# Opening of a two-layer encoder kernel: half of the first shift's weights multiplied with c on TensorE, and rows of u put ahead of the first weights' casts

## The chip, the cores and the metric

The kernel runs on one core of one Trainium2 chip. The metric is the device time of one execution in microseconds (us); lower is better. Besides the timed runs there is one profiled execution of the kernel, whose trace is read here. In the rows PE is TensorE (matrix products), PEld its weight loads, DVE is VectorE, ACT is ScalarE, POOL is GpSimd, and SP is the engine whose queue issues most transfers.

## What is computed

Two layers with three sub-layers each work on x (256 rows of 1024) under a conditioning vector c. Every sub-layer has a shift, a scale and a gate of 1024 numbers each, all of them products of silu(c) with a slice of `mod_w`:

```python
cs = jax.nn.silu(c)
for layer in range(DEPTH):
    mod = (cs @ mod_w[layer] + mod_b[layer]).reshape(bsz, N_SUB, 3, D_MODEL)
    x = adaln_sublayer(x, mod[:, 0], lambda u: 0.5 * swiglu(u, ffn_w_gate[layer, 0], ...), ...)
    ...

def adaln_sublayer(x, m, f, ln_g, ln_b):
    shift, scale, gate = m[:, None, 0], m[:, None, 1], m[:, None, 2]
    y = f(x * (1 + scale) + shift)
    return layer_norm(DEEPNORM_ALPHA * x + (1 + gate) * y, ln_g, ln_b)
```

The first sub-layer's f is a SwiGLU: silu(u @ w_gate) * (u @ w_up), times w_down. Nothing of it can start before u = x * (1 + scale) + shift is there, and that needs the whole scale and the whole shift of sub-layer 0.

## The kernel before

**The modulation.** `mod_gen` is a generator that walks through all slices of `mod_w`, for each sub-layer first scale (i = 1), then shift (i = 0), then gate (i = 2). A slice is 1024 x 1024 and comes in eight pieces k = 0 to 7, each 128 partitions by 1024. VectorE multiplies a piece by column k of c (`csT`) and adds it to an accumulator of 128 x 1024 (L219 for k = 0, L226 after that). When all eight are in, the partitions have still to be summed: `mod_cols0` does that with eight products on TensorE, in each of which a block of 128 x 128 of the accumulator is the loaded weight and a single column of ones is what moves through; so 1024 sums come out as eight columns of 128. In the trace each such fp32 product appears as two weight loads and two matmuls, so a group of eight products is "x16".

The first shift is a special case. Its piece k = 5 does not go over VectorE: TensorE multiplies it directly with column 5 of c (`self.share = self.mod_cols0(w, c)`, also eight products), two wide products that only keep TensorE active follow (`warm`, 512 columns each, result unused), and VectorE takes k = 0 to 4, 6 and 7. Then come the eight products with ones over the accumulator, in two PSUM banks in turn, and after each two of them VectorE adds their columns to B. `A` (scale + 1) and `B` (shift) are set by `mod_scale` and `mod_shift` behind VectorE's last accumulating step.

**The first u.** `make_u` with both row blocks (`joint`): TensorE turns x by products with the identity into four PSUM banks (L290). For each of four row groups of u (k0 = 0, 2, 4, 6) `affine` applies A and B, half on VectorE (L304) and half on ScalarE (L306), and `split` makes two fp32r parts of the result: a rounded copy on ScalarE (CAST, L266) and the rest by a subtraction on VectorE or GpSimd (L267). Three products of such parts stand for one fp32 product.

**The first weights.** `ffn` with `first == "start"` loads the first chunk of w_gate and w_up in two halves s = 0 and 1. The s = 0 halves are split in pieces of four k each, on ScalarE (cast) and GpSimd (subtraction): the two of w_gate at once where they stand in the program, the two of w_up from the list `between`, from which `make_u` takes one after each of the first two row groups. Then the products of chunk 0 start (L548), and after them chunk 1, whose w_up weights are loaded into a buffer that comes free when the s = 1 half of w_gate is split.

Each engine works off its instructions in the order in which they are recorded, and a scheduler chooses that order by what is ready; `behind(mark)` keeps an instruction behind another. Transfers go through SP's queue in order, each waiting until its buffer is free: `w8` (three buffers of 1 MB, the pairs of pieces and the FFN weights) and `wd` (three buffers of 512 KB, the single pieces and w_down).

Of the kernel before, what the change touches and what calls it, by code (L numbers as in the profile page):

```python
# [18 lines left out]
P = 128  # L19
# [14 lines left out]
class Trunk:  # L34
# [108 lines left out]
    def mod_cols0(self, acc, c, use=None):  # L143

        pts = [self.bank("gu", (P, KD)) for _ in range(2 if use else 1)]
        for k in range(KD):
            pt = pts[k // 2 % len(pts)]
            self.last_col = self.nc.tensor.matmul(pt[:, k : k + 1], acc[:, k * P : (k + 1) * P], c,
                                                  start=True, stop=True)
            if use and k % 2:  # L150
                use(slice(k - 1, k + 1), pt)
        return pts[0]
# [13 lines left out]
    def mod_shift(self, si, acc):  # L166
# [3 lines left out]
        if si == 0:  # L170
            self.mod_cols0(acc, self.one[:, 0:1], lambda c, pt: add(B[:, c], pt[:, c], B[:, c]))
        else:
            add(B, B, b)
            add(B, B, self.mod_cols(acc))
# [11 lines left out]
    def mod_gen(self):  # L186
# [4 lines left out]
        ws, loaded, G, step = {}, 0, None, None  # L191
# [14 lines left out]
        for n, (si, i, k) in enumerate(todo):  # L206
# [10 lines left out]
            w, c = ws.pop((si, i, k)), self.cs[:, k : k + 1]  # L217
            if k == 0:
                nc.vector.tensor_scalar_mul(acc, w, c)  # L219
            elif (si, i, k) == (0, 0, 5):  # L220
                self.share = self.mod_cols0(w, c)
                with self.behind(self.last_col):
                    for _ in range(2):
                        self.warm(self.x[:, 0, 0:512])
            else:
                step = nc.vector.scalar_tensor_tensor(acc, w, c, acc, ALU.mult, ALU.add)  # L226
# [3 lines left out]
            if self.last_mm is not None and self.si == 3:  # L230
# [3 lines left out]
                with self.behind(self.last_mm):  # L234
                    self.mod_sums(si, i, acc, G, step)
            else:
                self.mod_sums(si, i, acc, G, step)
            self.mdone.add((si, i))
            yield 0
            if si == 0 and i == 1:  # L240
                self.setup_bias()
                self.load_x()

    def mod_sums(self, si, i, acc, G, step):
# [7 lines left out]
        else:  # L252
            if not si:
                with self.behind(step):
                    self.mod_scale(si, self.scale)
                    self.nc.vector.tensor_tensor(out=self.AB[0][1], in0=self.share[:, 0:KD], in1=self.bcol[:, 0, 0],
                                                 op=ALU.add)
# [1288 lines left out]
```

## Time and profile before

| | before |
|---|---|
| median of 3 runs | 1204.01 us (1203.51 to 1205.42) |
| the profiled execution: time, span | 1207.6 us, 1205.8 us |
| PE busy | 1130.7 us, 94% of the span |
| DVE busy | 914.1 us, 76% |
| ACT busy | 548.5 us, 45% |
| POOL busy | 254.7 us, 21% |
| transfers | 259.74 MB, mean 215 GB/s |

The span is the time between the first and the last instruction in the trace; the time of the execution is a little longer. Busy shares are means over stages that have different limits, so the opening has to be read by itself: in the first 17 us TensorE does almost nothing.

### The profile page before, as it was taken

What the parts mean: (1) busy time and instruction counts of PE and PEld (TensorE: products, weight loads), DVE (VectorE), ACT (ScalarE), POOL (GpSimd) and SP (SyncE); (2) the same over time, 40 slices, a digit from 0 to 9 for tenths busy, and PEclk for the clock granted to TensorE, in tenths of its full rate; (3) what the DMA queues carried; (4) which work ended last, traced back from release to release, by engine and by line L of the source; (5) the groups of instructions that cost most, each with busy time, mean ns of one, the idle gap of its engine ahead of it and who ended that gap; (6) DMA issues with size and microseconds to landing.
All of it is one profiled execution on the core that took longest, in us unless ns stands there. A gap on an engine that the chain in (4) does not pass through costs nothing.

```text
span 1205.8 us, 19555 instructions
## 1 busy us (share of the span) xinstructions
PE 1130.7 (94%) x7703; PEld 1023.8 (85%) x7703; DVE 914.1 (76%) x1404; ACT 548.5 (45%) x963; POOL 254.7 (21%) x186
## 2 busy tenths in 40 slices
PE   4998999999799998999999899999898998999997
PEld 3887999789687887998999799999887878899995
DVE  6699777698886677878876778878799748866545
ACT  0644434356432445544443553444356656544430
POOL 0631000224731362230000332000121234400001
PEclk9998999999999999999999999999999998999999
DMA  9779998454310577689988388988733335885620
GB/s 354 256 255 327 314 318 294 142 181 132 106 36 1 192 258 231 205 286 300 323 291 302 98 275 291 301 300 281 257 129 124 112 105 192 295 259 174 214 73 35
DMA packets 155333, 259.74 MB, mean 215 GB/s; under 512 B 8813, under 2 KB 117354, under 8 KB 155242
## 3 DMA queue, kind: packets, MB, share of 16 engines
q1 hardware_dynamic: 155050, 258.45, 64.3%
q8 instruction: 60, 0.98, 0.3%
q14 instruction: 31, 0.25, 0.1%
q10 hardware_dynamic: 192, 0.05, 0.0%
HBM read 257.43 MB, written 1.05 MB: 214 GB/s over the span
## 4 chain that ended last, share of the span: by engine, by line
PE 61%; DVE 21%; DMA 7%; ACT 4%; issue 4%; POOL 3%; SPq 0%; POOLq 0%; DVEq 0%; ACTq 0%
PE gu L272 10%; PE gu L271 10%; PE gu L273 10%; PE acc L273 7%; PE acc L271 7%; PE acc L272 7%; DMA wd<-ffn_w_down 3%; DVE macc L226 2%; DVE g L267 2%; DMA wd<-mod_w 2%; DVE x L391 1%; DMA w<-ffn_w_up 1%; DVE u L267 1%; POOL hd L267 1%; DVE k L1043 1%
## 5 line engine op out<-in xcount | busy, mean ns | idle before, releaser
L226 DVE SCALAR_TENSOR_TENSOR macc<-wd,csT,macc 128x1024 f32<-128x1024 f32 x112 | 167.8, 1498 | 26.3 <-DMA wd<-mod_w 26.0
L271 PE MATMUL gu<-uT,g 128*128 128x256 f32 x640 | 181.3, 283 | 2.5 <-ACT sg L556 2.5
L273 PE MATMUL gu<-uT,g 128*128 128x256 f32 x640 | 181.4, 283 | 1.7 <-DVE g L267 1.7
L273 PE MATMUL gu<-uT,u 128*128 128x256 f32 x640 | 181.3, 283 | 1.0 <-DVE u L267 1.0
L271 PE MATMUL gu<-uT,u 128*128 128x256 f32 x640 | 181.2, 283 | 0.0
L272 PE MATMUL gu<-uT,u 128*128 128x256 f32 x640 | 181.2, 283 | 0.0
L272 PE MATMUL gu<-uT,g 128*128 128x256 f32 x640 | 181.1, 283 | 0.0
L266 ACT CAST hd<-wd 128x1024 fp32r<-128x1024 f32 x88 | 92.2, 1049 | 139.4 <-DMA wd<-ffn_w_down 127.0
L271 PE MATMUL acc<-hd,h 128*128 128x512 f32 x352 | 142.0, 403 | 1.9 <-ACT h L266 1.9
L273 PE MATMUL acc<-hd,h 128*128 128x512 f32 x352 | 138.9, 395 | 2.5 <-DVE h L267 2.5
L272 PE MATMUL acc<-hd,h 128*128 128x512 f32 x352 | 138.9, 394 | 0.0
L267 DVE TENSOR_TENSOR g<-w,g 128x1024 fp32r<-128x1024 f32 x86 | 118.2, 1377 | 26.6 <-ACT g L266 26.5
L271 PEld LDWEIGHTS gu<-uT,g 128*128 128x128 f32 x640 | 122.7, 192 | 4.6 <-ACT sg L556 3.2
L273 PEld LDWEIGHTS gu<-uT,g 128*128 128x128 f32 x640 | 122.7, 192 | 2.4 <-DVE g L267 2.4
L273 PEld LDWEIGHTS gu<-uT,u 128*128 128x128 f32 x640 | 122.9, 192 | 1.2 <-DVE u L267 1.2
L272 PEld LDWEIGHTS gu<-uT,g 128*128 128x128 f32 x640 | 122.7, 192 | 1.4
L272 PEld LDWEIGHTS gu<-uT,u 128*128 128x128 f32 x640 | 122.9, 192 | 0.0
L271 PEld LDWEIGHTS gu<-uT,u 128*128 128x128 f32 x640 | 122.9, 192 | 0.0
L267 DVE TENSOR_TENSOR u<-w,u 128x1024 fp32r<-128x1024 f32 x81 | 104.0, 1289 | 21.5 <-ACT u L266 21.1
L266 ACT CAST u<-w 128x1024 fp32r<-128x1024 f32 (+1 forms) x89 | 91.6, 1038 | 58.8 <-DMA w<-ffn_w_up 44.6
L267 POOL TENSOR_TENSOR hd<-wd,hd 128x1024 fp32r<-128x1024 f32 x32 | 86.6, 2712 | 149.0 <-ACT hd L266 149.0
L267 POOL TENSOR_TENSOR hl<-w,hl 128x1024 fp32r<-128x1024 f32 x28 | 72.7, 2607 | 202.6 <-ACT hl L266 202.1
(403 smaller groups left out, 2472.8 us busy)
## 6 DMA issues: line engine op xcount, KB each, us to landing
wd<-mod_w SPq DMA_DIRECT2D x130, 512.0 KB, 5.0
wd<-ffn_w_down SPq DMA_DIRECT2D x88, 512.0 KB, 4.7
w<-ffn_w_gate SPq DMA_DIRECT2D x43, 1024.0 KB, 8.4
w<-ffn_w_up SPq DMA_DIRECT2D x43, 1024.0 KB, 7.3
w<-hyb_w_in SPq DMA_DIRECT2D x16, 1024.0 KB, 5.9
w<-mod_w SPq DMA_DIRECT2D x7, 1024.0 KB, 7.5
w<-hyb_w_out SPq DMA_DIRECT2D x4, 1024.0 KB, 4.9
w<-mla_w_out SPq DMA_DIRECT2D x4, 1024.0 KB, 5.0
```

The lines of the kernel that those rows point to most:

```text
L226: step = nc.vector.scalar_tensor_tensor(acc, w, c, acc, ALU.mult, ALU.add)
L266: i = self.nc.scalar.copy(hi, src)
L267: return i, (eng or self.nc.vector).tensor_tensor(out=lo, in0=src, in1=hi.bitcast(F32), op=ALU.subtract)
L271: nc.tensor.matmul(out, lh, rh, start=first, stop=False)
L272: nc.tensor.matmul(out, lh, rl, start=False, stop=False)
L273: self.last_mm = nc.tensor.matmul(out, ll, rh, start=False, stop=last)
L391: V.tensor_tensor(out=x[:, b, sl], in0=tmp, in1=x[:, b, sl], op=ALU.add)
L1043: nc.vector.scalar_tensor_tensor(y[:, d:], pt[:, : S - d], tap(3 - d), y[:, d:], ALU.mult, ALU.add)
```

## The change

Pieces k = 4 to 7 of the first shift go over TensorE instead of VectorE. A new function `mod_direct` makes eight products for each: the piece is the weight that is loaded, column k of c moves, and the results add up in PSUM in two banks. VectorE keeps k = 0 to 3; its accumulator goes into the same banks by eight products with ones, ahead of k = 4. After each two products of k = 7 VectorE adds the bias into B. The separate share of k = 5, its two wide products and the closing eight products with ones are gone. `mod_scale` for sub-layer 0 moves up behind `setup_bias`, one wide product stands behind the last column instead of two, and all four splits of the first weights now stand behind row groups of u: one after the first, two after the second, one after the third.

```diff
--- before.py
+++ after.py
@@ -140,16 +140,25 @@
             nc.vector.tensor_reduce(out=out[:, k0 : k0 + 4], in_=pt, op=ALU.add, axis=AX.X)
         return out
 
-    def mod_cols0(self, acc, c, use=None):
-
-        pts = [self.bank("gu", (P, KD)) for _ in range(2 if use else 1)]
+    def mod_cols0(self, acc, c):
+
+        pt = self.bank("gu", (P, KD))
         for k in range(KD):
-            pt = pts[k // 2 % len(pts)]
-            self.last_col = self.nc.tensor.matmul(pt[:, k : k + 1], acc[:, k * P : (k + 1) * P], c,
-                                                  start=True, stop=True)
-            if use and k % 2:
-                use(slice(k - 1, k + 1), pt)
-        return pts[0]
+            self.nc.tensor.matmul(pt[:, k : k + 1], acc[:, k * P : (k + 1) * P], c, start=True, stop=True)
+        return pt
+
+    def mod_direct(self, w, c, first, last):
+
+        nc = self.nc
+        if first:
+            self.direct = [self.bank("gu", (P, KD)) for _ in range(2)]
+        for k in range(KD):
+            pt = self.direct[k // 2 % 2]
+            self.last_col = nc.tensor.matmul(pt[:, k : k + 1], w[:, k * P : (k + 1) * P], c, start=first and k in (0, 2),
+                                             stop=last, skip_group_check=True)
+            if last and k % 2:
+                two = slice(k - 1, k + 1)
+                nc.vector.tensor_tensor(out=self.AB[0][1][:, two], in0=pt[:, two], in1=self.bcol[:, 0, 0, two], op=ALU.add)
 
     def mod_scale(self, si, sums):
         nc = self.nc
@@ -167,11 +176,8 @@
         nc = self.nc
         B, b = self.AB[si][1], self.bcol[:, si, 0]
         add = lambda out, x, y: nc.vector.tensor_tensor(out=out, in0=x, in1=y, op=ALU.add)
-        if si == 0:
-            self.mod_cols0(acc, self.one[:, 0:1], lambda c, pt: add(B[:, c], pt[:, c], B[:, c]))
-        else:
-            add(B, B, b)
-            add(B, B, self.mod_cols(acc))
+        add(B, B, b)
+        add(B, B, self.mod_cols(acc))
 
     def mod_gate(self, si, acc, G):
 
@@ -188,7 +194,7 @@
         nc, t = self.nc, self.t
         self.AB, self.G = {}, {}
         todo = [(si, i, k) for si in range(len(self.subs)) for i in (1, 0, 2) for k in range(KD)]
-        ws, loaded, G, step = {}, 0, None, None
+        ws, loaded, G = {}, 0, None
 
         def load(si, i, k):
             l, j = self.subs[si]
@@ -215,15 +221,15 @@
                 load(*todo[loaded])
                 loaded += 1
             w, c = ws.pop((si, i, k)), self.cs[:, k : k + 1]
+            direct = (si, i) == (0, 0) and k >= KD // 2
             if k == 0:
                 nc.vector.tensor_scalar_mul(acc, w, c)
-            elif (si, i, k) == (0, 0, 5):
-                self.share = self.mod_cols0(w, c)
-                with self.behind(self.last_col):
-                    for _ in range(2):
-                        self.warm(self.x[:, 0, 0:512])
+            elif direct:
+                self.mod_direct(w, c, False, k == KD - 1)
             else:
-                step = nc.vector.scalar_tensor_tensor(acc, w, c, acc, ALU.mult, ALU.add)
+                nc.vector.scalar_tensor_tensor(acc, w, c, acc, ALU.mult, ALU.add)
+            if (si, i, k) == (0, 0, KD // 2 - 1):
+                self.mod_direct(acc, self.one[:, 0:1], True, False)
             yield 1
             if k < KD - 1:
                 continue
@@ -232,16 +238,17 @@
                 self.held = self.last_mm
                 yield 0
                 with self.behind(self.last_mm):
-                    self.mod_sums(si, i, acc, G, step)
+                    self.mod_sums(si, i, acc, G)
             else:
-                self.mod_sums(si, i, acc, G, step)
+                self.mod_sums(si, i, acc, G)
             self.mdone.add((si, i))
             yield 0
             if si == 0 and i == 1:
                 self.setup_bias()
+                self.mod_scale(0, self.scale)
                 self.load_x()
 
-    def mod_sums(self, si, i, acc, G, step):
+    def mod_sums(self, si, i, acc, G):
         if i == 2:
             self.mod_gate(si, acc, G)
         elif i == 1:
@@ -249,12 +256,7 @@
                 self.mod_scale(si, self.mod_cols(acc))
             else:
                 self.scale = self.mod_cols0(acc, self.one[:, 0:1])
-        else:
-            if not si:
-                with self.behind(step):
-                    self.mod_scale(si, self.scale)
-                    self.nc.vector.tensor_tensor(out=self.AB[0][1], in0=self.share[:, 0:KD], in1=self.bcol[:, 0, 0],
-                                                 op=ALU.add)
+        elif si:
             self.mod_shift(si, acc)
 
     def need(self, *key):
@@ -315,14 +317,13 @@
             next(self.todo[0])
             self.need(si, 0)
             with self.behind(self.last_col):
-                for _ in range(2):
-                    self.warm(n[:, 0, 0:512])
-            for k0 in range(0, KD, 2):
-                with self.behind(self.marks[1]):
+                self.warm(n[:, 0, 0:512])
+            for k0, weights in zip(range(0, KD, 2), ((0,), (2, 1), (3,), ())):
+                with self.behind(*self.marks[1:2]):
                     affine(k0, pts[k0 // 2])
-                if k0 < 4:
+                for i in weights:
                     with self.behind(self.marks[1]):
-                        self.marks[1:] = self.between[k0 // 2]()
+                        self.marks[1:] = self.between[i]()
         else:
             for k0 in range(0, KD, 2):
                 affine(k0, rows(k0))
@@ -518,10 +519,7 @@
                             continue
                         for k in (slice(0, 4), slice(4, 8)):
                             piece = lambda hl=hl, r=r, k=k: self.split(hl[:, 0, k], hl[:, 1, k], r[:, k], nc.gpsimd)
-                            if g:
-                                self.between.append(piece)
-                            else:
-                                self.marks[1:] = piece()
+                            self.between.append(piece)
                     if not s:
                         yield
             u = self.u
```

On TensorE the place is the opening, between the transposes of x and the first products of chunk 0. `gu` are PSUM banks, `x` the input, `G` the accumulator, `w` and `wd` pieces of weights, `uT` the first u. Before:

```order
L125 MATMUL gu_146<-x_118,ident 128x512
L148 MATMUL gu_156<-csT,w_23_153 128x1 [waits DMAHW6_49]
L148 MATMUL gu_156<-csT,w_23_153 128x1 x7
L125 MATMUL gu_165<-x_118,ident 128x512 [waits Activation_49]
L125 MATMUL gu_167<-x_118,ident 128x512 [waits PE_49]
L148 MATMUL gu_195<-one,G_120 128x1 [waits DVE_49,PE_49]
...
L125 MATMUL gu_209<-x_118,ident 128x512
L125 MATMUL gu_211<-x_118,ident 128x512
L548 MATMUL gu_243<-uT_124,g_184 128x256 [waits DVE_49,Activation_49]
```

And in the changed kernel, with the rows between the first two of each group of eight left out:

```order
L125 MATMUL gu_149<-x_121,ident 128x512
L157 MATMUL gu_156<-one,G_123 128x1 [waits DVE_49]
...
L157 MATMUL gu_156<-csT,w_27_166 128x1 [waits DMAHW6_49]
...
L157 MATMUL gu_156<-csT,wd_184 128x1 [waits DMAHW7_49]
...
L157 MATMUL gu_156<-csT,wd_194 128x1 [waits DMAHW0_49]
...
L125 MATMUL gu_220<-x_121,ident 128x512 [waits PE_49]
L546 MATMUL gu_256<-uT_127,g_217 128x256 [waits PE_49,Activation_49]
```

Two groups of eight narrow products with four wide ones among and behind them became five groups of eight without a wide one among them, and one wide product behind.

On VectorE the place is the first shift's accumulation. Before (the rows from the end of the scale's accumulation on):

```order
L226 SCALAR_TENSOR_TENSOR G_81<-w_8_94,csT,G_81 128x1024 [waits DVE_49]
L219 TENSOR_SCALAR G_120<-w_14_121,csT 128x1024 [waits DMAHW4_49]
L226 SCALAR_TENSOR_TENSOR G_120<-w_14_121,csT,G_120 128x1024 [waits DVE_49]
L226 SCALAR_TENSOR_TENSOR G_120<-w_22_149,csT,G_120 128x1024 [waits DMAHW5_49,DVE_49]
L226 SCALAR_TENSOR_TENSOR G_120<-w_22_149,csT,G_120 128x1024 [waits DVE_49]
L226 SCALAR_TENSOR_TENSOR G_120<-w_23_153,csT,G_120 128x1024 [waits DMAHW6_49,DVE_49]
L226 SCALAR_TENSOR_TENSOR G_120<-wd_169,csT,G_120 128x1024 [waits DMAHW7_49,DVE_49]
L226 SCALAR_TENSOR_TENSOR G_120<-wd_172,csT,G_120 128x1024 [waits DMAHW0_49,DVE_49]
L158 SCALAR_TENSOR_TENSOR A_191<-gu_98,bcol 128x8 [waits Activation_49]
```

And now:

```order
L230 SCALAR_TENSOR_TENSOR G_81<-w_8_94,csT,G_81 128x1024 [waits DVE_49]
L167 SCALAR_TENSOR_TENSOR A_118<-gu_98,bcol 128x8 [waits Activation_49]
L226 TENSOR_SCALAR G_123<-w_16_124,csT 128x1024 [waits DMAHW4_49]
L230 SCALAR_TENSOR_TENSOR G_123<-w_16_124,csT,G_123 128x1024 [waits DVE_49]
L230 SCALAR_TENSOR_TENSOR G_123<-w_24_152,csT,G_123 128x1024 [waits DMAHW5_49,DVE_49]
L230 SCALAR_TENSOR_TENSOR G_123<-w_24_152,csT,G_123 128x1024 [waits DVE_49]
L161 TENSOR_TENSOR B_119<-gu_156,bcol 128x2 [waits PE_49]
```

Three accumulating steps are gone, and the step that makes A, which waits for ScalarE's copy of the bias columns (`bcol`), stands ahead of the four that are left.

On ScalarE the place is the first row groups of u. Before:

```order
L95 COPY bcol<-gu_114 128x96 [waits PE_49]
L266 CAST g_184<-w_31_181 128x512 [waits DMAHW1_49]
L266 CAST g_184<-w_31_181 128x512
L306 ACTIVATE tmp_213<-acc_125,B_192,A_191 128x256 [waits DVE_49,PE_49]
L266 CAST uT_124<-tmp_213 128x512 [waits Activation_49]
L266 CAST u_190<-w_32_182 128x512 [waits DMAHW2_49]
```

And now:

```order
L95 COPY bcol<-gu_114 128x96 [waits PE_49]
L308 ACTIVATE tmp_222<-acc_128,B_119,A_118 128x256 [waits DVE_49,PE_49]
L268 CAST uT_127<-tmp_222 128x512 [waits Activation_49]
L268 CAST g_217<-w_32_214 128x512 [waits DMAHW1_49]
L308 ACTIVATE tmp_229<-acc_133,B_119,A_118 128x256 [waits DMAHW4_49,DMAHW5_49,DMAHW3_49,DMAHW6_49,DMAHW0_49,DMAHW7_49,DVE_49,PE_49]
```

The two casts of w_gate's first half (`g`) moved from ahead of the first row group of u to behind the first and among the second.

## Rows read from the trace of the kernel before

**Rows 1.** Chain of work that ended last, 0 to 140 us (start, us, what).

```profile
17.06 3.57 PE gu L148 x16
20.90 3.41 PE acc L290 x16
24.31 1.71 PE gu L125 x2
26.02 1.87 PE gu L148 x16
27.89 1.82 PE gu L125 x4
29.71 1.69 PE gu L148 x16
...
37.88 2.42 POOL g L267
40.32 0.38 SPq L450
```

**Rows 2.** Instructions in order of time, opening, VectorE with its releasers, and bcol.

```profile
19.39 0.75 DVE L219 TENSOR_SCALAR G<-w,csT 128x1024 f32<-128x1024 f32 x1 [2.38 <-DMA w<-mod_w]
...
20.93 0.24 ACT L95 COPY bcol<-gu 128x96 f32<-128x96 f32 x1 [18.50 <-PE gu L93]
...
22.02 3.93 DVE L226 SCALAR_TENSOR_TENSOR G<-w,csT,G 128x1024 f32<-128x1024 f32 x3 [0.56 <-DMA w<-mod_w]
...
25.99 2.61 DVE L226 SCALAR_TENSOR_TENSOR G<-wd,csT,G 128x1024 f32<-128x1024 f32 x2
...
28.51 0.16 DVE L158 SCALAR_TENSOR_TENSOR A<-gu,bcol 128x8 f32<-128x8 f32 x1
...
30.53 0.16 DVE L169 TENSOR_TENSOR B<-gu,B 128x2 f32<-128x2 f32 x1 [0.29 <-PE gu L148]
```

**Rows 3.** The same view: ScalarE's and GpSimd's first casts and subtractions.

```profile
28.96 1.14 ACT L266 CAST g<-w 128x512 fp32r<-128x512 f32 x2 [7.78 <-DMA w<-ffn_w_gate]
...
29.66 2.49 POOL L267 TENSOR_TENSOR g<-w,g 128x512 fp32r<-128x512 f32 x2 [28.37 <-ACT g L266]
...
31.25 0.56 ACT L306 ACTIVATE tmp<-acc,B,A 128x256 f32<-128x256 f32 x1 [1.15 <-DVE B L169]
...
32.37 0.61 ACT L266 CAST u<-w 128x512 fp32r<-128x512 f32 x1
32.89 0.56 ACT L306 ACTIVATE tmp<-acc,B,A 128x256 f32<-128x256 f32 x1
...
33.06 3.35 POOL L267 TENSOR_TENSOR u<-w,u 128x512 fp32r<-128x512 f32 x2 [0.91 <-ACT u L266]
```

**Rows 4.** Weight load of the share of k = 5, same view as rows 2.

```profile
24.96 0.34 PEld L148 LDWEIGHTS gu<-csT,w 128*128 128x128 f32 x1 [0.52 <-DMA w<-mod_w]
```

**Rows 5.** Busy us by engine (PE, PEld, DVE, ACT, POOL), PEclk, DMA share, GB/s.

```profile
17.00:24.00 7.00, 6.94 (x33) 6.94 (x34) 3.98 (x5) 0.24 (x1) 0.00 (x0) 1.00 1.03 410
...
25.00:26.00 1.00, 1.00 (x4) 0.48 (x2) 0.96 (x2) 0.00 (x0) 0.00 (x0) 1.00 1.01 406
...
27.00:28.00 1.00, 1.00 (x9) 1.00 (x10) 0.96 (x2) 0.00 (x0) 0.00 (x0) 1.00 1.21 290
```

**Rows 6.** The same view where the granted clock falls, around 98 us.

```profile
94.50:97.90 3.40, 0.08 (x1) 0.00 (x0) 3.37 (x5) 0.00 (x0) 1.78 (x1) 1.00 1.02 352
97.90:104.70 6.80, 5.87 (x10) 3.35 (x11) 3.98 (x8) 3.08 (x5) 0.00 (x0) 0.51 1.07 370
```

**Rows 7.** The same view where it falls around 258 us.

```profile
255.00:258.40 3.40, 1.18 (x11) 0.94 (x10) 3.40 (x7) 2.26 (x3) 0.00 (x0) 1.00 0.78 229
258.40:261.80 3.40, 3.40 (x18) 3.40 (x17) 3.36 (x11) 0.21 (x1) 2.55 (x1) 0.50 0.25 83
```

**Rows 8.** The same view for the stages behind the opening.

```profile
40.00:66.00 26.00, 24.28 (x179) 22.78 (x178) 18.02 (x21) 13.81 (x19) 12.39 (x7) 1.00 0.77 263
66.00:98.00 32.00, 27.56 (x206) 26.18 (x204) 31.49 (x51) 10.67 (x15) 14.68 (x38) 1.00 0.74 247
```

## The prediction

> **What bounds the opening now.** I read the chain of work that ended last first [rows 1]. From 17.06 us to 31.4 us it is TensorE without a break: the eight products that sum the scale, the transposes of x, one wide product, the eight products for k = 5, two wide products, and the eight products that sum the shift, which end at 29.71 + 1.69 = 31.40 us. Behind them comes the first row group of u, and the chain goes on over GpSimd's subtraction for w_gate's second half (37.88 us) to SP, which can only then issue a weight load (40.32 us). So what counts in this stage is when TensorE ends the last column of the shift, not when VectorE does.
>
> The instructions in order of time show the two engines that feed it. VectorE starts the first shift at 19.39 us, when its first weights land, and ends its last accumulating step at 28.60 us [rows 2]; its second addition into B is at 30.53 us, and ScalarE's first row group of u starts 0.72 us after that, at 31.25 us [rows 3]. The weights are not late: those of k = 4 and 5 have landed at 24.96 us [rows 4], and the transfer rate falls from 406 to 290 GB/s between 26 and 27 us, where the FFN weights follow the last `mod_w` pieces [rows 5]. So all eight pieces of the shift are in by about 27 us. What remains after that is arithmetic.
>
> **What a group of eight narrow products costs.** The chain has the same 16 records three times, at three prices [rows 1]: 3.57 us at 17.06, 1.87 us at 26.02 and 1.69 us at 29.71. The transposes, also 16, take 3.41 us. The column of the granted clock reads 1.00 over all of it [rows 5], but a price that halves without any wait is TensorE going from the 1.2 to the 2.4 GHz level, and it happens at about 26 us, right after the first wide product. Before that TensorE was busy 6.94 of 7.00 us with narrow products and transposes and stayed at the lower level [rows 5]. That is the row to keep in mind: what TensorE did before the clock rose was a product of 512 columns, and seven busy microseconds of weight loads and narrow columns ahead of it went by at the lower level.
>
> **The change part by part.**
>
> *Three accumulating steps leave VectorE* (k = 4, 6, 7, at 1.31 us each, 3.93 / 3 [rows 2]): 3.9 us. They are worth something only if TensorE gets to its last column sooner.
>
> *The step that makes A moves ahead of them.* It waits for bcol, which is there at 20.93 + 0.24 = 21.17 us. So VectorE, which began the shift at 19.39 us, now begins at about 21.35 us and ends k = 3 at 21.35 + 0.75 + 3.93 = 26.0 us [rows 2] instead of 24.65. TensorE comes out of its wide product at 26.02 us in any case [rows 1]. This costs nothing (bound: 0.1 us), with the wide product as its cover; without that it would be 1.4 us.
>
> *TensorE now does five groups instead of two.* The first can start at about 26.1 us. The data for the others are in by then or soon after, so the groups run one behind the other. At the higher level throughout: 26.1 + 1.87 + 4 x 1.69 = 34.7 us, 3.3 us later than 31.40. VectorE's saved steps cost 1.31 us a piece, their replacements 1.69, and TensorE was the engine on the chain already. At the lower level throughout: 26.1 + 5 x 3.41 = 43.15 us. These are the two bounds.
>
> *The wide products are gone from between the groups.* Nothing in the trace shows over 8 us of narrow products at the higher level, so which bound is nearer has to come from the neighbouring rows. The granted clock falls to 0.50 at 97.9 us, after 3.4 us in which TensorE did nothing [rows 6], and at 258.4 us after 3.4 us in which it was busy 1.18 us [rows 7]. [...] I put the fall in the changed kernel as far behind its last wide product, at 26.0 + 3.4 = 29.4 us. By then 1.87 us for the first group and (29.4 - 27.97) / 1.69 = 0.85 of the second are done; 3.15 groups at 3.41 us make 10.7 us; the last column ends at 40.1 us. VectorE's second addition stands half a group earlier: 38.4 us against 30.53. The first row group of u starts 0.72 us behind, at 39.1 us: **+7.9 us**.
>
> The Trainium skill ("TensorE: Matmul & The Clock Gate", section on LDWEIGHTS) has a weight load take its number of columns over 1.2, 107 ns for 128, with no word of the clock. By that the five groups take 80 x 107 ns = 8.6 us at either level, which is my upper-level bound. The trace agrees at 29.71 us (1.69 / 16 = 106 ns) and not at 17.06 us (223 ns), and the measurement decides.
>
> *Two casts move behind row groups of u on ScalarE.* Before, w_gate's first half was cast at 28.96 us while ScalarE waited for B anyway [rows 3]; it was free. Now both casts stand among the row groups, each a step of 0.52 us (32.37 to 32.89 [rows 3]), so the cast of w_gate's second half and all behind it moves by 1.05 us against the first row group. GpSimd's four pieces now run in one stretch behind it; they took 2.49 / 2 = 1.25 us each alone and 3.35 / 2 = 1.68 us beside VectorE's subtractions, so GpSimd may end up to 1.8 us later instead. I take **+1.05 us**, since GpSimd has idle time behind.
>
> *What is late next.* The second half's subtraction on GpSimd releases the buffer for chunk 1's w_up, and SP's queue stands behind it [rows 1]; a transfer of w_down now also waits for TensorE to be done with the piece k = 6, ahead of chunk 1's w_gate in the same queue, but the transfers before it have work until after 33 us. Between 40 and 98 us TensorE is busy 24.28 of 26.00 and VectorE 31.49 of 32.00 us [rows 8]: there is hardly idle time in which a late start could be made up, so I carry the delay to the end in full.
>
> **Sum.** 7.9 + 1.05 = about +9.0 us on the profiled execution's 1207.6 us, of which 1.8 us lie outside its span: 1216.6. The profiled execution is 3.6 us above the median of the timed runs; on that median, 1204.0 + 9.0 = **1213.0 us**.
>
> **The rivals.**
> *The level holds.* Then the last column ends at 34.7 us, the first row group starts 3.3 us later, and with 1.05 us the time is 1208.4. For it: TensorE has no gap at all in the stretch, and weight loads keep it busy. The Trainium skill speaks for it too (same page, "Why this matters for your kernels"): it wants TensorE kept busy without idle gaps between bursts, and here is none. Against it: the stretch at 17 to 24 us, busy and slow [rows 5]. Chance 0.20.
> *It never rises.* It rose after one wide product among transposes, with another narrow group behind; if that is borderline, all five groups run at the lower level: 43.15 us, second addition at 41.4, row group at 42.1, +10.9 + 1.05 = 1216.0. Chance 0.20.
> *The products follow the landings.* With each piece multiplied as it lands, only one group is left after about 27 us, so the last column ends near 28.7 us, 2.7 us earlier, and less 1.05 us that is 1202.4, faster. It decides on whether TensorE reaches k = 7 with nothing queued; that needs the four groups before it done in the 0.9 us from 26.1 to 27 us, some 0.2 us each, against 1.69 in the row. Chance 0.05.
> *The delay is made up later.* TensorE waits for VectorE up to 98 us, and if that wait is set by loads rather than by work, the late opening vanishes: 1204. Against it the same 31.49 of 32.00 us. Chance 0.05.
>
> **How the numbers follow.** My forecast, the fall in the midst of the stretch, has 0.50; alone it would run from 1210.5 to 1215.5, by where the level falls and whether GpSimd adds its 0.8 us. The range reaches to the rival where the level holds (1208.4, less 1 us that may be made up) and to the one where it never rises (1216.0, plus 0.8 us): 1207.2 to 1217.0, which leaves the two last rivals and some tails, 0.15. A measurement of this kernel can tell about 0.2% (2.4 us) from no change. Slower than that: 0.90; within it: 0.06; faster: 0.04, the part of the landing rival beyond it and unknowns.
>
> **What the trace would show.** Right: on TensorE five groups back to back from about 26 us; the first two at about 1.7 us, the later ones at 3.4; a granted clock of 0.50 somewhere between 29 and 45 us; ScalarE's first row group near 39 us, and chunk 0's first products past 40 us. Groups of 1.7 us to the end and a first row group near 34.6 us would mean that the level holds. VectorE's last step of the shift should end near 26 us; if it ends much later, the wait for bcol costs what I booked as nothing. Wrong altogether would be a first row group before 31 us, or the same shift at 40 us gone at 100 us.

## The result, and the profile after

| | before | changed |
|---|---|---|
| median of 4 runs each | 1204.22 us (1203.51 to 1205.42) | 1217.27 us (1215.16 to 1219.44) |
| profiled execution: time, span | 1207.6, 1205.8 us | 1219.44, 1217.7 us |
| PE, DVE, ACT, POOL busy | 94, 76, 45, 21% | 94, 75, 45, 21% |

The changed kernel is slower: ratio 1.0100, 95% interval 1.0083 to 1.0117; that is 12.0 us (10.0 to 14.1), and the medians stand 13.05 us apart. I had forecast 1213.0 us, with 1217.0 as the upper end; the measured median lies 0.3 us above that end. The busy shares of the page hardly moved; nearly all of the loss arises in the opening.

First the chain of work that ended last in the changed kernel (start, us, what), which answers to [rows 1]:

```profile
18.58 3.57 PE gu L147 x16
...
27.57 15.82 PE gu L157 x80
...
69.52 8.84 DMA w<-ffn_w_up
...
111.57 3.40 PE gu L187 x4
```

Where before the chain had 5.38 us of TensorE from the share to the last column (26.02 to 31.40 us), it has 80 records in 15.82 us now. That is 198 ns a record on the mean, against 106 to 117 in the two groups of before, so most of these went by at the lower level of TensorE's clock.

The instructions in order of time, in the same kernel, show how that came about:

```profile
22.45 0.24 ACT L95 COPY bcol<-gu 128x96 f32<-128x96 f32 x1 [19.85 <-PE gu L93]
22.72 0.17 DVE L167 SCALAR_TENSOR_TENSOR A<-gu,bcol 128x8 f32<-128x8 f32 x1 [4.20 <-ACT bcol L95]
...
23.59 3.93 DVE L230 SCALAR_TENSOR_TENSOR G<-w,csT,G 128x1024 f32<-128x1024 f32 x3
...
25.62 1.09 PE L125 MATMUL gu<-x,ident 128*128 128x512 f32 x2
...
27.57 2.15 PE L157 MATMUL gu<-one,G 128*128 128x1 f32 x16 [0.86 <-DVE G L230]
...
29.58 6.96 PE L157 MATMUL gu<-csT,w 128*128 128x1 f32 x32
...
36.41 6.96 PE L157 MATMUL gu<-csT,wd 128*128 128x1 f32 x32
...
42.42 0.56 ACT L308 ACTIVATE tmp<-acc,B,A 128x256 f32<-128x256 f32 x1 [19.73 <-DVE tmp L306]
...
53.55 0.38 SPq L451 DMA_DIRECT2D w<-ffn_w_up  x1
```

The same wide product in the same view of the kernel before:

```profile
24.10 1.92 PE L125 MATMUL gu<-x,ident 128*128 128x512 f32 x2
```

Three things are to be seen. VectorE waits for `bcol` before it begins the shift at all, and its last accumulating step ends at 23.59 + 3.93 = 27.52 us. The wide product that was to cover this took 1.09 us and not 1.92 (the 1.71 of [rows 1] count from the end of the transposes), because TensorE reached the higher level as it began and not behind it, so TensorE was done at 26.71 us and waited 0.86 us for VectorE. And of the five groups only the first (2.0 us, to 29.58) is anywhere near the higher price; the other four take 13.79 us, 3.45 us each.

The windows (PE, PEld, DVE, ACT, POOL busy us, PEclk, DMA share, GB/s) have the clock beside it:

```profile
25.30:28.60 3.30, 2.44 (x15) 1.61 (x13) 2.17 (x2) 0.00 (x0) 0.00 (x0) 1.00 0.84 293
28.70:35.00 6.30, 6.30 (x34) 6.30 (x33) 0.00 (x0) 0.00 (x0) 0.00 (x0) 0.54 1.07 285
29.10:29.20 0.10, 0.10 (x3) 0.10 (x2) 0.00 (x0) 0.00 (x0) 0.00 (x0) 0.81 0.70 138
35.00:43.40 8.40, 8.40 (x41) 8.40 (x41) 0.93 (x4) 0.95 (x2) 0.00 (x0) 0.50 0.41 139
43.40:49.00 5.60, 5.21 (x17) 3.89 (x18) 5.54 (x7) 5.41 (x11) 4.21 (x4) 0.50 0.43 145
49.20:55.00 5.80, 5.80 (x49) 5.80 (x48) 5.74 (x4) 3.74 (x6) 4.71 (x3) 0.96 0.07 7
```

The level falls at about 29.16 us: between 29.10 and 29.20 us the clock is 0.81 on the mean. TensorE is busy 8.40 of 8.40 us from 35 us on and has a granted clock of 0.50, the 1.2 GHz level, all the while. It is back at the higher level only at about 49.6 us, among chunk 0's products of 256 columns, so the first of these pay the lower price too. The Trainium skill ("TensorE: Matmul & The Clock Gate", "Why this matters for your kernels") wants TensorE busy without idle gaps. Here TensorE has no gap from 27.57 to 43.39 us; the clock fell 1.6 us into that stretch and did not rise again in it, so the trace disagrees with that rule for a stretch of weight loads and single columns.

The way of the delay: ScalarE's first row group of u starts 11.17 us later (31.25 [rows 3] to 42.42), the first gate product (the sums over gate's accumulator, `macc`) 12.74 us later (98.83 to 111.57), and the end of the span is 11.9 us later. In the kernel before that product is this row:

```profile
98.83 2.05 PE L181 MATMUL gu<-macc,one 128*128 128x512 f32 x2 [4.25 <-DVE macc L226]
```

Of the 11.17 us, 1.52 belong to this execution: the products that sum the scale began at 18.58 us instead of 17.06 [rows 1], because VectorE had waited 1.30 us for weights ahead of its last two steps of the scale. In the traces of all kernels here that start lies between 16.9 and 18.6 us.

### The profile page after: what moved, and what is told of

The parts are those of the page before. It is cut to its first block, busy times and chain, and to the rows that moved or that the text cites. A ratio compares the mean times of both kernels' runs of the same rounds, so it can differ in the third digit from the quotient of the medians.

```text
span 1217.7 us, 19632 instructions
## 1 busy us (share of the span) xinstructions
PE 1141.7 (94%) x7745; PEld 1037.1 (85%) x7745; DVE 913.1 (75%) x1400; ACT 547.4 (45%) x963; POOL 255.1 (21%) x186
## 3 DMA queue, kind: packets, MB, share of 16 engines
HBM read 257.43 MB, written 1.05 MB: 212 GB/s over the span
## 4 chain that ended last, share of the span: by engine, by line
PE 64%; DVE 19%; DMA 7%; ACT 5%; issue 3%; POOL 2%; SPq 0%; POOLq 0%; DVEq 0%; ACTq 0%
PE gu L275 10%; PE gu L274 10%; PE gu L273 10%; PE acc L275 8%; PE acc L273 7%; PE acc L274 7%; DMA wd<-ffn_w_down 2%; DVE g L269 2%; DVE macc L230 2%; DMA wd<-mod_w 2%; DMA w<-ffn_w_up 2%; PE gu L157 1%; DVE u L269 1%; DMA w<-mod_w 1%; DVE x L392 1%
## 5 line engine op out<-in xcount | busy, mean ns | idle before, releaser
L269 DVE TENSOR_TENSOR u<-w,u 128x1024 fp32r<-128x1024 f32 x81 | 107.0, 1327 | 21.6 <-ACT u L268 21.4
```

The source lines that it names most:

```text
L269: return i, (eng or self.nc.vector).tensor_tensor(out=lo, in0=src, in1=hi.bitcast(F32), op=ALU.subtract)
```

## The experiments

My theory after the result had three parts: five groups of narrow products at the lower level for most of their length; the wait for `bcol`, which I had booked at nothing; and the moved casts, booked at 1.05 us. The rivals were that the missing wide products are the whole loss (then putting them back heals it), that the casts are, and that the first profile shows a chance execution. Each line below gives a median and beside it the median of the kernel before on the same chip; the interval in brackets is of the ratio, and 0.0010 of it are 1.2 us.

**The change once more (`after_again`).**

> The changed kernel once more, beside the runs that follow. In its profiled execution the scale's sum began 1.5 us later than in the kernel before because weights landed later. Theory: that was this one execution; here the sum begins near 17.0 us and the time is some 1.0 us lower against the kernel before than the first 13 us (plus 11 to 13 us). Rival: it belongs to the kernel, and the sum begins near 18.6 us again.

1217.35 us against 1205.16, ratio 1.0096 (1.0082 to 1.0110), +12.2 us. The scale sum began at 18.08 us and the columns at 27.06 us, 9.0 us behind it just as in the first profile; the first row group of u stood at 42.37 us. So the course repeats. Two things vary: the start of the scale sum, and the fall of the level, which came at about 28.15 us (granted clock 1.00 up to 28.10, 0.50 from 28.20 us on), 1.1 us behind the start of the columns and not 1.6.

**Wide products back between the groups, one each (`e1_wide_between`).**

```diff
             if (si, i, k) == (0, 0, KD // 2 - 1):
                 self.mod_direct(acc, self.one[:, 0:1], True, False)
+                with self.behind(self.last_col):
+                    self.warm(self.x[:, 0, 0:512])
...
                 self.mod_direct(w, c, False, k == KD - 1)
+                if k < KD - 1:
+                    with self.behind(self.last_col):
+                        self.warm(self.x[:, 0, 0:512])
```

> The changed kernel with one more wide product (512 columns, result unused) behind each of the first four groups of eight narrow products. Theory, the clock: nearly all of the loss is TensorE at the lower level in the five groups (15.8 us for 80 records in the changed kernel). With wide products among them the level holds, a group takes 1.7 to 1.9 us and a wide product 0.9, together 5 x 1.75 + 4 x 0.9 = 12.4 us, so the last column ends some 3.5 us earlier than in the changed kernel and the time is about 1213.5 us (1212 to 1215). Rival, the amount of work: the level doesn't matter here, five groups are simply too much; then four wide products only add 3.6 us or more, and the time is 1221 us or above.

1224.52 us against 1205.43, ratio 1.0155 (1.0142 to 1.0169): slower still. The instructions in order of time, and a window over the stretch:

```profile
25.93 1.95 PE L157 MATMUL gu<-one,G 128*128 128x1 f32 x16 [0.41 <-DVE G L233]
...
28.92 3.41 PE L157 MATMUL gu<-csT,w 128*128 128x1 f32 x16
...
32.19 2.05 PE L125 MATMUL gu<-x,ident 128*128 128x512 f32 x2
...
34.04 3.41 PE L157 MATMUL gu<-csT,w 128*128 128x1 f32 x16
```

```profile
28.00:48.30 20.30, 20.30 (x73) 16.21 (x73) 1.45 (x6) 1.53 (x3) 0.00 (x0) 0.51 0.62 179
```

One product of 512 columns behind each eight narrow ones did not hold the level: it fell at about 28.4 us, in spite of the product, and then the wide products cost 1.85 us each as well (32.19 to 34.04 us). My forecast, that they would keep the level, was wrong.

**Two each (`e5_two_wide_between`).** The same edit with `for _ in range(2):` around each wide product.

> The changed kernel with two wide products behind each of the first four groups, as the kernel before has them behind its share. One did not hold the level. Theory, the level: with two it holds, every group takes 1.7 to 1.9 us and every pair of wide products 1.9 us, so the columns take 5 x 1.75 + 4 x 1.9 = 16.3 us as against 15.8 without any, although 8 wide products are added; chunk 0 begins at the higher level; the time is within 2 us of the changed kernel's. Rival, the amount of work: the groups stay at 3.4 us and each pair adds 3.7 us, the columns take 31 us, and the time is 15 us above the changed kernel's.

1223.0 us against 1205.16, ratio 1.0145 (1.0128 to 1.0161). Here the level held, as instructions and window show:

```profile
28.58 1.96 PE L125 MATMUL gu<-x,ident 128*128 128x512 f32 x4
30.38 1.84 PE L157 MATMUL gu<-csT,w 128*128 128x1 f32 x16
32.08 1.96 PE L125 MATMUL gu<-x,ident 128*128 128x512 f32 x4
```

```profile
27.00:42.70 15.70, 15.70 (x97) 11.88 (x97) 0.84 (x4) 0.11 (x1) 0.00 (x0) 1.00 0.70 199
```

With two wide products a group costs 1.7 us instead of 3.4, and the two cost 1.8 us: nothing is won or lost. The columns took 16.0 us (26.77 to 42.73), as forecast, against 15.8 without any wide product. So in this execution the level was bought, at about what it gave. The time did not follow: 5.7 us above the changed kernel where I had allowed 2. The distance from the first row group of u to the first gate product is 71.01 us here instead of 69.2; where the rest arises I have not traced. In this version the weights of a later chunk were issued in another order; that this order is the cause was not tested.

**The casts where they were (`e2_casts_back`), and the casts alone (`e3_casts_alone`).** The first puts the old order of the splits back into the changed kernel; the second puts the new order into the kernel before.

```diff
-            for k0, weights in zip(range(0, KD, 2), ((0,), (2, 1), (3,), ())):
-                with self.behind(*self.marks[1:2]):
+            for k0 in range(0, KD, 2):
+                with self.behind(self.marks[1]):
...
-                            self.between.append(piece)
+                            if g:
+                                self.between.append(piece)
+                            else:
+                                self.marks[1:] = piece()
```

> The changed kernel with the four splits of the first weights where they stood before (w_gate's two at once, w_up's one behind each of the first two row groups of u). Theory: the moved casts cost 1.05 to 1.8 us, so this is 1215.4 to 1216.2 us where the changed kernel is 1217.3. Rival: they are hidden (TensorE and VectorE are late anyway), and the time stays at 1217.3 within 0.4.

> The kernel before with only the new order of the splits (one behind the first row group of u, two behind the second, one behind the third). Theory: plus 1.05 to 1.8 us, 1205.3 to 1206.0 us. Rival: hidden, 1204.2 us. If the casts were the main part of the loss, it would be above 1210 us.

`e2_casts_back`: 1214.70 us against 1205.43, ratio 1.0077 (1.0065 to 1.0089), +9.3 us where the changed kernel has +12.2 on another chip. By the medians the casts cost about 2.9 us in the changed kernel, more than the 1.05 to 1.8 that I had. The trace puts less of it down to them. In order of time on TensorE, and in two windows:

```profile
25.91 1.95 PE L157 MATMUL gu<-one,G 128*128 128x1 f32 x16 [1.30 <-DVE G L230]
27.71 4.89 PE L157 MATMUL gu<-csT,w 128*128 128x1 f32 x32
32.47 6.97 PE L157 MATMUL gu<-csT,wd 128*128 128x1 f32 x32
```

```profile
25.90:29.90 4.00, 4.00 (x36) 4.00 (x36) 0.00 (x0) 1.13 (x2) 0.43 (x1) 1.00 1.10 285
30.00:39.40 9.40, 9.40 (x46) 9.40 (x45) 0.93 (x4) 0.89 (x2) 1.96 (x2) 0.50 0.81 236
```

Up to the last column TensorE has the same instructions here as in the changed kernel, but the level fell at 30.0 us, 4.1 us behind the start of the columns instead of 1.6 and 1.1, and the columns took 13.53 us instead of 15.82 and 16.26. In `e11_products_alone` below the casts are back too and the fall comes early, so that gain is not shown to be the casts'. What goes with the casts is the distance from the first row group of u to the first gate product: 67.24 us here and 67.51 in `e11_products_alone`, against 69.15 and 69.21 in the changed kernel. By this they cost 1.6 to 2.0 us.

`e3_casts_alone`: 1205.56 us against 1205.43, ratio 1.0005 (0.9996 to 1.0014). No change is seen where I had forecast 1.05 to 1.8 us, but the interval reaches 1.7 us and so excludes little of that; in its trace the distance is 67.97 us, 0.4 more than before. That the casts are better hidden beside the opening of the kernel before is likely and not shown. Which wait makes the difference I have not isolated.

**The kernel before without wide products (`e4_no_wide`).** All four are taken out, those behind the share and those behind the last column.

> The kernel before without the two wide products behind the share of k = 5 and without the two behind the last columns; the one behind the transposes stays. Theory, the clock: the level falls near the closing group, which then takes up to 3.4 us instead of 1.7, and chunk 0 begins at the lower level; plus 1 to 4 us, 1205 to 1208 us. Rival, the amount of work: wide products only stand in the way on the engine that is the path; the closing group starts at 28.7 instead of 29.7 us, and the time is about 1203.2 us.

1207.05 us against 1205.43, ratio 1.0012 (1.0003 to 1.0021): +1.6 us, inside the 1 to 4 forecast. On TensorE, in order of time, and in a window around the fall:

```profile
26.02 2.16 PE L148 MATMUL gu<-csT,w 128*128 128x1 f32 x16
28.71 2.29 PE L148 MATMUL gu<-one,G 128*128 128x1 f32 x16 [0.53 <-DVE B L253]
```

```profile
29.70:36.40 6.70, 4.84 (x23) 4.45 (x23) 6.04 (x11) 6.12 (x12) 4.99 (x4) 0.53 1.14 335
```

The level fell at about 30.1 us here too, but only the end of the second group was left by then. So all four wide products are worth 1.6 us (0.4 to 2.5), and the change removed three of them; the larger loss comes with the three added groups, most of which stand behind the fall. Chunk 0's last two products began 2.7 us later (47.76 us against 45.02), yet the first gate product stood at 98.87 us, where it was; where the 1.6 us arise behind it stays open.

**A behind VectorE's last step, as before (`e6_scale_behind`).**

```diff
-                nc.vector.scalar_tensor_tensor(acc, w, c, acc, ALU.mult, ALU.add)
+                step = nc.vector.scalar_tensor_tensor(acc, w, c, acc, ALU.mult, ALU.add)
             if (si, i, k) == (0, 0, KD // 2 - 1):
+                with self.behind(step):
+                    self.mod_scale(0, self.scale)
...
                 self.setup_bias()
-                self.mod_scale(0, self.scale)
```

> The changed kernel with the step that makes A behind VectorE's last accumulating step, as before. I booked its move as nothing; in the changed kernel's trace TensorE waits 0.9 us for VectorE ahead of the first group. Theory: the columns begin 0.9 to 1.3 us earlier, and the time is 0.9 to 2 us lower than the changed kernel's (more than the wait, since what is done earlier is done at the higher level). Rival: TensorE is not ready earlier, or the level falls earlier by the same; no change within 0.4 us.

1214.58 us against 1205.16, ratio 1.0074 (1.0057 to 1.0091): 2.8 us below the changed kernel on the same chip, more than the 0.9 to 2 forecast. In order of time on TensorE:

```profile
25.49 1.84 PE L157 MATMUL gu<-one,G 128*128 128x1 f32 x16
...
27.20 6.34 PE L157 MATMUL gu<-csT,w 128*128 128x1 f32 x32
...
33.40 6.96 PE L157 MATMUL gu<-csT,wd 128*128 128x1 f32 x32
```

The first group stands without a wait, 7.77 us behind the start of the scale sum instead of 8.99. The other part is the level: it fell 2.4 us behind the start of the columns instead of 1.6 and 1.1, so more of them went by before the fall, and they took 14.87 us instead of 15.82 and 16.26. Together the first row group of u comes 2.2 to 2.6 us earlier against the scale sum (21.69 us behind it instead of 23.84 and 24.29). The 2.8 us are a difference of two medians whose intervals overlap, so the trace is the better measure.

**Two pieces on TensorE instead of four (`e8_three_groups`).** `direct` from `k >= KD - 2`, the eight products with ones behind k = 5; VectorE takes k = 0 to 5.

> The changed kernel with only k = 6 and 7 on TensorE directly (three groups of eight instead of five), k = 0 to 5 on VectorE. Theory, groups at the lower level: VectorE ends k = 5 at 28.7 us, three groups take 5.1 us at the higher and 10.2 us at the lower level, and with the level falling ahead of or in the first of them the last column ends at 36 to 39 us instead of 42; the time is 3 to 6 us lower than the changed kernel's. Rival: the number of groups is not what costs (the moved casts and the queue behind them are); then it stays within 1.5 us of the changed kernel.

1215.09 us against 1205.16, ratio 1.0073 (1.0059 to 1.0087): 2.3 us below the changed kernel, not 3 to 6. In order of time:

```profile
28.83 3.58 PE L157 MATMUL gu<-one,G 128*128 128x1 f32 x16 [2.99 <-DVE G L230]
...
32.27 6.97 PE L157 MATMUL gu<-csT,wd 128*128 128x1 f32 x32
```

Two groups fewer would be 6.9 us at 3.45, but now TensorE waits 2.99 us for VectorE, the level falls at the end of that wait, and all three groups go at the lower price.

**What is late next (`e9_swap`), with one wide product fewer (`e7_one_wide`, `e10_swap_one_wide`).** In the prediction I had named GpSimd's subtraction for w_gate's second half, behind which SP's queue stands, as the way by which the delay goes on. `e9_swap` gives it to VectorE, in the kernel before.

```diff
-                                self.split(hl[:, 0], hl[:, 1], r, (nc.gpsimd, None)[g])
+                                self.split(hl[:, 0], hl[:, 1], r, (None, nc.gpsimd)[g])
```

> The kernel before with the second halves' subtractions exchanged: w_gate's on VectorE, w_up's on GpSimd. In every trace so far the gate of the first sub-layer is multiplied 57.4 to 59.4 us after SP can issue chunk 1's w_up (except with two wide products, 60.4), and that issue waits for w_gate's second half to be subtracted. Theory, this wait is the path: VectorE ends it at about 39.2 us instead of 40.3, and the time is 1.1 us lower, 1204.0 us where the kernel before is 1205.1. Rival: it is not the path but moves along with it; the issue comes earlier and the gate product doesn't, no change.

> The kernel before with one wide product behind its share instead of two (the two behind the last columns stay). In its trace the second one ends 0.5 to 1 us after VectorE is done, so the closing group waits for it. Theory: the closing group and all behind it come 0.9 us earlier, 1204.2 us where the kernel before is 1205.1. Rival, from the run in which one wide product per group didn't hold the level: the level falls ahead of the closing group or of chunk 0, and the time is 1 to 3 us higher, 1206 to 1208 us.

> Both: one wide product behind the share, and the exchanged subtractions. Theory: the two add up, 2.0 us lower than the kernel before, 1203.1 us where that is 1205.1. Rival: one wide product lets the level fall, and the sum is 1205 to 1207 us.

`e9_swap`: 1205.70 us against 1205.76, ratio 0.9998 (0.9986 to 1.0010). In order of time:

```profile
38.14 1.23 DVE L267 TENSOR_TENSOR g<-w,g 128x1024 fp32r<-128x1024 f32 x1 [0.26 <-ACT g L266]
...
39.44 0.38 SPq L450 DMA_DIRECT2D w<-ffn_w_up  x1
...
98.88 3.75 PE L181 MATMUL gu<-macc,one 128*128 128x512 f32 x4 [4.19 <-DVE macc L226]
```

The load that stood behind the subtraction is issued 7.9 us behind the first row group of u instead of 9.1, and the first gate product stays 67.3 us behind it (67.6 before). So to shorten that wait is worth nothing by itself. It does not take GpSimd off the path, though: the exchange gives GpSimd the second half of w_up instead, and the chain of work that ended last then runs from there over GpSimd's subtractions for w_down (`hd`) to the load of chunk 2's w_up. In `e9_swap`:

```profile
39.13 0.93 POOL u L267
...
41.62 4.45 POOL hd L267 x2
...
50.66 3.40 POOL hd L267
...
56.06 9.27 DMA w<-ffn_w_up
```

And in the kernel before:

```profile
50.21 3.41 POOL hd L267
...
55.67 9.63 DMA w<-ffn_w_up
```

The last subtraction and the load stand where they stood, about 19 and 24.5 us behind the first row group of u. Whether GpSimd's work as a whole is what carries the delay on was not tested.

One wide product instead of two behind the share: 1205.96 us against 1205.76, ratio 1.0001 (0.9991 to 1.0011). Both: 1205.67, ratio 0.9997 (0.9986 to 1.0009). With one wide product the level fell at about 31 us, behind the closing group, and was back at about 34 us; but it did so in `e3_casts_alone` with two wide products as well, so one product fewer is not shown to be the reason. None of the versions beats the kernel before.

**The products alone (`e11_products_alone`).** The edits of `e2_casts_back` and `e6_scale_behind` together: of the change only the five groups and the missing wide products are left.

> The changed kernel with both side edits undone (the four splits where they stood, and the step that makes A behind VectorE's last accumulating step): what is left of the change is that TensorE multiplies k = 4 to 7 itself. Theory, three terms that add up: undoing one of them alone took 2.7 us each, so this is about 5.4 us under the changed kernel, 6 to 7.5 us above the kernel before (1211.5 to 1213), all of it the five groups mostly at the lower level. Rival: the two edits overlap (both shorten the same wait), and it is only 3 us under the changed kernel, 9 to 10 us above the kernel before.

1213.25 us against 1206.29, ratio 1.0059 (1.0043 to 1.0075), +7.0 us (5.2 to 9.0), as the parts added up (6 to 7.5). In order of time:

```profile
25.52 1.95 PE L157 MATMUL gu<-one,G 128*128 128x1 f32 x16
...
27.33 6.53 PE L157 MATMUL gu<-csT,w 128*128 128x1 f32 x32
...
33.72 6.96 PE L157 MATMUL gu<-csT,wd 128*128 128x1 f32 x32
```

## Why the prediction was right in direction and too low

The accounts of the +12.2 to +13.05 us, each part from the run that undoes it: 7.0 us the groups on TensorE (`e11_products_alone`), 2.8 us the place of the step that makes A (`e6_scale_behind`), 2.9 us the moved casts (`e2_casts_back`). Undoing the last two together gives 5.2 us (12.2 - 7.0), a little less than the 5.7 of the two apart. Each part is a difference of medians of four to six runs, uncertain by about 2 us either way; the traces put A at 2.2 to 2.6 and the casts at 1.6 to 2.0 us.

- **Three steps leave VectorE.** Right: they were worth nothing, as `e8_three_groups`, which gives two of them back, is 2.3 us lower than the changed kernel.
- **The step that makes A, booked at nothing.** This is the step that failed in its mechanism; the two that are called mis-sized below had theirs right. I had the wait for `bcol` right and its 1.4 us without cover too, but took the wide product for a cover of fixed length. It shrank by 0.83 us (1.92 to 1.09) with the clock, and TensorE stood idle for 0.86 us, in `after_again` for 1.10. Without the move the first group starts 1.2 us earlier against the scale sum (7.77 us behind it instead of 8.99). The forecast start, 9.04 us behind it (26.1 - 17.06), was met all the same, but by luck: the clock rose earlier than in the kernel before, and the wait took what that gave.
- **Five groups, at two prices.** Right: 1.7 and 3.4 us, with the fall in their midst. Mis-sized: I had 3.3 us between the first group's start and the fall, and measured 1.6 us (27.57 to 29.16), in `after_again` 1.1. Half of the difference is the wait just named, which went by at the higher level; the other half is that the fall came 2.45 us behind the wide product (26.71 to 29.16), in `after_again` 2.2, and not 3.4. Each such us puts 0.6 of a group from 1.7 to 3.4 us and so costs another us: against the scale sum the first row group of u is 9.65 and 10.1 us later than in the kernel before (23.84 and 24.29 us behind it instead of 14.19), forecast 7.9. The distance to the fall is no constant: in `e2_casts_back` it is 4.1 us behind the first group's start.
- **The groups without the wait.** In `e11_products_alone` the last column ends at 40.69 us, forecast 40.1, and the first row group of u stands at 39.73, forecast 39.1; what the forecast booked for this, 7.9 us, measures 7.0. That agreement is luck in part: against the scale sum the groups begin 1.4 us earlier than forecast there, and the level falls 2.3 us behind their start and not 3.3.
- **The two casts, +1.05 us.** Mis-sized: 1.6 to 2.0 us in the traces of the changed kernel, 2.9 by the medians. The load of chunk 1's w_up is issued 11.1 us behind the first row group of u (42.42 to 53.55) where it was 9.1 before (31.25 to 40.32) and is 9.3 with the casts back, so GpSimd's subtraction ahead of it is late by about 2 us and not by 1.05. In the kernel before no price was seen (`e3_casts_alone`).
- **What is late next.** The wait for GpSimd's subtraction of w_gate's second half is not by itself the path (`e9_swap`); GpSimd's later work is not ruled out. In all traces but that of `e5_two_wide_between` the first gate product stands 42.0 to 43.2 us behind the issue of chunk 2's w_up (69.52 us in the chain above). That fits a path over this load and was not tested alone.
- **Carried to the end in full.** Right: 11.2 us at the first row group of u, 12.7 at the first gate product, 11.9 at the end of the span.

So of the 3 to 4 us by which the forecast of +9.0 us was too low, 1.7 to 2.2 are the wait and the earlier fall and about 0.5 to 1 the casts. The rest, 0 to 1.8 us by the profile that is taken, is no larger than the spread of the start of the scale sum and is not settled. The terms that the range names end at 1207.4 (1208.4 - 1) and 1216.8 us (1216.0 + 0.8), 0.2 us inside the bounds that I gave.

The rivals: that the level holds is refuted by the windows; `e5_two_wide_between` shows a course in which it did. That it never rises gave the nearest price (1216.0), by a course that did not happen: the clock rose earlier than before, and fell. That the products follow the landings, and that the delay is made up later, are refuted by the chain.

The Trainium skill's rule on weight loads ("TensorE: Matmul & The Clock Gate", section on LDWEIGHTS) counts 1 ns for 1.2 columns and names no clock; by an estimate from its figure, 41 loads of 128 columns take 4.4 us. The window from 35.00 to 43.40 us has 41 in 8.40 us, nearly all with one narrow product each, so the trace disagrees with it at the lower level.

## What to carry to other kernels

Work moved from an engine that is off the chain to the one that is on it cost its full price here, and for eight products that each load 128 x 128 fp32 weights for one column that price is 1.7 or 3.4 us, by the level of the clock; five such groups one behind another did not keep the higher level to their end in any run here. Where an edit is booked at nothing because other work covers it, ask what the cover costs at the other level: the wide product was 0.83 us shorter here than in the row that I had taken it from. And where the moment at which the level falls differs between executions, check what two medians say by the stretch of the trace that the edit touches: the casts cost 2.9 us by the medians and 1.6 to 2.0 by their stretch.

## What the runs showed of the hardware that was not expected

- TensorE busy without any gap (8.40 of 8.40 us) at a granted clock of 0.50: through weight loads and single columns the higher level neither lasted nor came back. With one fp32 product of 512 columns behind each eight narrow ones the clock was 0.51 over 20 us; with two it was 1.00 over 15.7 us, one execution each.
- The moments at which the clock rises and falls differ between executions. The wide product behind the transposes took 1.92 us in the kernel before, and 1.02 us in `e3_casts_alone`, which has the same instructions on TensorE up to there. With the same products on TensorE the fall came 1.1, 1.6 and 4.1 us behind the first group's start (`after_again`, the first profile of the changed kernel, `e2_casts_back`).
- The start of the scale sum, before which no changed instruction stands, differs between executions by up to 1.7 us (16.9 to 18.6 us); in the latest of them VectorE had waited 1.30 us for weights.
